# An encoder trunk on one core: the order of all instructions planned with other landing times and durations

## The chip, the cores and the metric

The kernel runs on one core of one Trainium2 chip. A core has a TensorE (PE) for matmuls, a VectorE (DVE), a ScalarE (ACT), a GpSimd (POOL) and a SyncE (SP) that here only issues DMAs. The metric is device time in microseconds (us) of one execution; less is better.

## The reference

Two layers work on x of 256 tokens by 1024. Each is an FFN, a mixer and an FFN, with a layer norm behind each part. The mixer of layer 0 is a bidirectional mLSTM, that of layer 1 a windowed attention with grouped queries.

```python
def swiglu(x, w_in, w_out):
    gu = x @ w_in
    g, u = gu[..., :D_FF], gu[..., D_FF:]
    return (jax.nn.silu(g) * u) @ w_out
...
    for l in range(DEPTH):
        x = layer_norm(ALPHA * x + 0.5 * swiglu(x, ffn_w_in[l, 0], ffn_w_out[l, 0]), ln_g[l, 0], ln_b[l, 0])
        j = l // N_MIXERS
        if l % N_MIXERS == 0:
            y = mlstm_mixer(x, ml_w_in[j], ml_gate_b[j], ml_norm_g[j], ml_w_out[j])
        else:
            y = window_attention(x, at_w_in[j], at_sink[j], at_w_out[j])
        x = layer_norm(ALPHA * x + y, ln_g[l, 1], ln_b[l, 1])
        x = layer_norm(ALPHA * x + 0.5 * swiglu(x, ffn_w_in[l, 1], ffn_w_out[l, 1]), ln_g[l, 2], ln_b[l, 2])
```

All of it is float32, with D_FF = 2816.

## The kernel before

**Products.** A float32 product is made of three matmuls: each operand is split into a high part (a rounded copy, made by ACT, `w_hi` for weights) and a low part (the rest, made by DVE, `w_lo`), and high by high, high by low and low by high are added up in PSUM. Many blocks of the FFN's first product take seven products in place of eight; they need sums of weight blocks. Some of these sums DVE makes (`b <- b, b`), others a DMA makes that adds what it brings to what lies in the tile: 80 accumulating DMAs, all issued by POOL, 512 KB each. A weight tile that was filled that way then goes through ACT (`w_hi <- b`) and DVE (`w_lo <- b, w_hi`) to PE. Plain loads are issued by SP.

**Other names.** `x_69` and `x_70` are the two token tiles of x (called x0 and x1 below). `xT_hi` and `xT_lo` are their transposes, made by PE with `ident` and split by ACT and DVE. A norm takes sums on DVE, the squares on ACT (`sq, sums <- x, sums`), `rs <- sums` on DVE, `rs <- rs, few` on POOL, and two steps on DVE: `x <- x, sums, ln_g` and `x <- x, rs, ln_b`. `h_hi` and `h_lo` are the FFN's inner activation, `e` an evacuated part of a seven-product block, `S` a sum of x's blocks, `q_hi`, `q_lo`, `pr` and `pv` belong to attention.

**The order.** The kernel's text doesn't issue instructions. It notes steps in a `Book`, and `order` plans them: `cost` (L328) gives each step the time that it takes and the time after which its result is seen; `latest` walks from the end and gives each step a due time by what needs it on PE; `sequence` then goes through time and gives each engine, out of the first 16 candidates, one that can start soonest and is due first. For that it must believe when a DMA has landed: `rings.add` models the two queues, with constants in `RING`, `PACKET` and `SUMMED` (L64 to L66), and sets `steps[n_].lands`; `wait_for` decides whether an engine waits a little for a more urgent step. PE's order is that of the text. `sequence` also picks the buffer slot of each tile (10 slots for high parts, 10 for low, 16 for raw weights), so another order gives other slots. `emit` issues the planned list, so that nearly every row of the profile has its line, L597. On the chip every engine runs its own list in order, and waits for semaphores where an operand isn't there yet: a step whose DMA is late holds all that stand behind it on its engine.

Of the kernel before, what the change touches and what calls it, by code (L numbers as in the profile page):

```python
# [11 lines left out]
F32 = mybir.dt.float32  # L12
# [48 lines left out]
LOADING = 1400.0  # L61
ADDING = 5500.0
QUEUED = 6000.0
RING = {"SP": (2000.0, 600.0), "POOL": (2900.0, 1500.0)}  # L64
PACKET = {4096: 162.0, 2048: 88.0, 1024: 48.6}
SUMMED = 163.0  # L66
HELD = 13
PRESSING = 800.0
EARLY = 60000.0
# [96 lines left out]
class Rings:  # L166
# [9 lines left out]
    def run(self, until):  # L176
# [8 lines left out]
        while True:  # L185
# [23 lines left out]
            if not c.left[step]:  # L209
                del c.left[step]  # L210
                if done is not None:
                    done[step] = c.t + RING[q][1]

    def add(self, s, extra=0.0):
# [3 lines left out]
        if q == "POOL":  # L218
            n, each = 16, SUMMED
        else:  # L220
            size = 4 * s.args[1].shape[-1]
            n = max(1, int(np.prod(s.args[0].shape)) * 4 // size // 16)
            each = PACKET.get(size, size / 23.0) + extra / n
        self.jobs[q].append((s.start + RING[q][0], n, each, s.n))
        self.left[s.n] = n
# [24 lines left out]
class Book:  # L250
# [77 lines left out]
    def cost(self, s):  # L328

        size = lambda v: int(np.prod(v.shape[1:]))  # L330
        n = max([size(v) for v in s.outs + s.ins], default=0)
        if s.engine == "PE":
            n = size(s.outs[0])
            s.takes, s.later = (109.0 if s.name == "transpose" else n / 2.4 + 13.3), 200.0
            narrow = s.name == "matmul" and s.args[1].shape[0] == 64
            if narrow:
                s.takes = 58.5
            if narrow != self.narrow:
                s.takes, self.narrow = s.takes + (195.0 if narrow else 146.0), narrow
        elif s.name == "dma_start":  # L340
            s.takes = {"SP": ISSUE, "ACT": 480.0, "POOL": 1250.0}[s.engine]
            s.later = 0.0
        elif s.engine == "DVE":
            psum = any(v.room.kind == "bank" for v in s.ins)
            s.takes, s.later = (n + 71) / 0.96, 120.0
            if s.name == "scalar_tensor_tensor":
                s.takes += 55.0
                if "accum_out" in s.kw:
                    s.takes += 90.0
            if psum and s.outs[0].dtype is F32:  # L350
                s.takes += 60.0
            if s.name == "tensor_add" and s.outs[0].shape[0] == 64:
                s.takes += 30.0
            if s.name == "tensor_tensor_scan":
                s.takes = 710.0
            if s.name == "tensor_tensor_reduce":
                s.takes = 405.0
            if s.name == "bn_stats":
                s.takes = 728.0 if n == 512 else 335.0
            if s.name == "bn_aggr":  # L360
                s.takes = 244.0 if n > 6 else 115.0
        elif s.engine == "ACT":
            s.takes, s.later = n * 0.912 + 17.0, 125.0
            if s.name.startswith("preload"):
                s.takes = 1290.0
            if s.name == "activation" and s.args[2] is not AF.Copy:
                s.takes += 48.0
            if any(isinstance(s.kw.get(k), View) for k in ("bias", "scale")):
                s.takes += 110.0
            if "accum_out" in s.kw:  # L370
                s.takes, s.later = s.takes + 93.0, 215.0
        else:
            s.later = 80.0
            s.takes = {"tensor_tensor": 1500.0, "partition_broadcast": 1100.0, "iota": 600.0,
                       "affine_select": 1600.0}.get(s.name, n * 0.93 + 100.0)
            if s.name == "tensor_add":
                s.takes = 2150.0 if n >= 512 else 1000.0
            if s.name == "tensor_scalar":
                s.takes = 460.0 if n > 64 else 200.0
# [41 lines left out]
    def sequence(self):  # L421
        steps = self.steps
        state = {}
        for kind, rooms in self.rooms.items():
            first, last = np.array([r.first for r in rooms] or [0]), np.array([r.last for r in rooms] or [0])
            n = len(rooms)
# [49 lines left out]
        while len(given) < len(steps):  # L476
            best = None
            for e, list_ in todo.items():
# [7 lines left out]
                for n in cands:  # L486
                    s = steps[n]
# [20 lines left out]
            t, _, n, e = best  # L508
            s = steps[n]
# [8 lines left out]
            if s.name == "dma_start":  # L518
                if e == "POOL" and s.kw.get("accum_op") is None:
                    s.lands = s.end + LANDING + LOADING  # L520
                elif loads < len(RAMP):
                    dma = s.lands = RAMP[loads]
                    rings.t = dma - RING[e][1]
                    loads += 1
                else:
                    for n_, t_ in rings.add(s).items():
                        steps[n_].lands = t_
                        if steps[n_].engine == "SP":
                            dma = max(dma, t_) if n_ == n else dma
                    loads += 1  # L530
# [1084 lines left out]
```

## Time and profile before

| what | us |
|---|---|
| median of 3 runs | 906.04 |
| lowest and highest of them | 904.73, 907.65 |
| the profiled execution | 904.83 |
| its span in the profile | 903.1 |

The profile shows one execution. "Busy" is the time in which an engine runs an instruction; a step's row gives its start, its duration, engine, line, operation and tiles, and in brackets the idle time ahead of it with what ended that. PE's matmuls are pipelined, so the end of one lies behind the start of the next, and stalls are read from the distance of starts. An accumulating DMA shows on POOL only as the 1.2 us in which it is issued; when it landed is told by the table of DMA issues.

### The profile page before, as it was taken

The numbers are of one execution on the slowest core, as the hardware profiler recorded it, in microseconds if no ns is written. First come the engines' busy times: TensorE is split into PE (matmuls) and PEld (weight loads), VectorE is DVE, ScalarE is ACT, GpSimd is POOL, SyncE is SP. The second block draws the span as 40 slices with busy tenths as digits, with TensorE's granted clock in tenths as the row PEclk, the third lists the DMA queues.
The fourth block names the chain that finished last, engine by engine and source line by source line (L and its number), as shares of the span: only waits on it lengthen the run. The fifth ranks groups of instructions, "written<-read, shape, count | busy, mean of one in ns | idle before, by whom it ended". The sixth has DMA issues, their size and how long they took to land.

```text
span 903.1 us, 12618 instructions
## 1 busy us (share of the span) xinstructions
PE 892.5 (99%) x4387; PEld 744.3 (82%) x4387; DVE 815.9 (90%) x1008; ACT 635.1 (70%) x881; POOL 157.8 (17%) x194
## 2 busy tenths in 40 slices
PE   9999999999999999999999999999999999999996
PEld 7888888889988888888888888887898788888885
DVE  7999998678797999999879999996889899999975
ACT  7777677657665886776679776776788777677650
POOL 0121221014012221112011221131033131112100
PEclk9999999999999999999999999999999999999999
DMA  9999998844395989999966999999534588999931
GB/s 317 380 306 273 274 317 243 293 141 141 119 315 149 212 241 316 300 249 278 363 185 177 244 291 322 295 258 347 168 113 113 168 191 230 306 267 263 307 90 46
DMA packets 106111, 216.92 MB, mean 240 GB/s; under 512 B 7192, under 2 KB 23600, under 8 KB 106048
## 3 DMA queue, kind: packets, MB, share of 16 engines
q1 hardware_dynamic: 84000, 174.09, 54.6%
q0 software_dynamic: 22048, 42.04, 27.1%
q8 instruction: 34, 0.56, 0.2%
q14 instruction: 29, 0.24, 0.1%
HBM read 215.04 MB, written 1.05 MB: 239 GB/s over the span
## 4 chain that ended last, share of the span: by engine, by line
PE 73%; DVE 11%; issue 9%; DMA 5%; ACT 1%; POOL 1%; DVEq 0%; POOLq 0%; ACTq 0%
PE pw L597 45%; PE py L597 28%; DVE w_lo L597 5%; DMA b<-in_ffn_w_in_dram 5%; DVE b L597 2%; DVE x L597 1%; DVE e L597 1%; ACT w_hi L597 1%; POOL b L597 1%; POOL rs L597 1%; DVE S L597 0%; DVE xT_lo L597 0%; DVE pv L597 0%; DVE sc L597 0%; DVE h_lo L597 0%
## 5 line engine op out<-in xcount | busy, mean ns | idle before, releaser
L597 ACT CAST w_hi<-b 128x1024 fp32r<-128x1024 f32 x266 | 277.6, 1053 | 98.6 <-PE py L597 45.4
L597 DVE TENSOR_TENSOR w_lo<-b,w_hi 128x1024 fp32r<-128x1024 f32 x266 | 317.5, 1220 | 9.9 <-ACT w_hi L597 9.8
L597 DVE TENSOR_TENSOR w_lo<-raw,w_hi 128x1024 fp32r<-128x1024 f32 (+1 forms) x158 | 187.4, 1208 | 10.5 <-ACT w_hi L597 9.1
L597 PE MATMUL pw<-w_hi,S 128*128 128x512 f32 x608 | 195.3, 391 | 0.2 <-ACT e L597 0.2
L597 ACT CAST w_hi<-raw 128x1024 fp32r<-128x1024 f32 (+1 forms) x158 | 163.2, 1042 | 44.3 <-PE py L597 19.1
L597 POOL DMA_DIRECT2D b<-in_ffn_w_in_dram x80 | 97.0, 1218 | 497.4 <-DVE b L597 173.8
L597 PE MATMUL pw<-w_hi,xT_hi 128*128 128x512 f32 (+1 forms) x420 | 164.9, 394 | 0.4 <-ACT xT_hi L597 0.4
L597 PE MATMUL pw<-w_hi,xT_lo 128*128 128x512 f32 (+1 forms) x420 | 162.4, 388 | 0.0
L597 PE MATMUL pw<-w_lo,xT_hi 128*128 128x512 f32 (+1 forms) x420 | 161.2, 387 | 0.0
L597 PEld LDWEIGHTS pw<-w_hi,S 128*128 128x128 f32 x608 | 114.2, 188 | 25.0 <-ACT e L597 0.7
L597 PE MATMUL py<-w_hi,h_hi 128*128 128x512 f32 x317 | 125.7, 397 | 0.0
L597 PE MATMUL py<-w_hi,h_lo 128*128 128x512 f32 x317 | 124.0, 391 | 0.6 <-DVE h_lo L597 0.6
L597 PE MATMUL py<-w_lo,h_hi 128*128 128x512 f32 x317 | 123.5, 390 | 0.0
L597 PE MATMUL pw<-w_lo,S 128*128 128x512 f32 x304 | 118.4, 390 | 0.0
L597 PEld LDWEIGHTS pw<-w_hi,xT_lo 128*128 128x128 f32 x420 | 78.9, 188 | 18.3 <-DVE xT_lo L597 2.1
L597 PEld LDWEIGHTS pw<-w_hi,xT_hi 128*128 128x128 f32 x420 | 79.0, 188 | 16.2 <-ACT xT_hi L597 1.4
L597 PEld LDWEIGHTS pw<-w_lo,xT_hi 128*128 128x128 f32 x420 | 78.9, 188 | 14.6
L597 DVE TENSOR_TENSOR b<-b,b 128x1024 f32<-128x1024 f32 x72 | 87.7, 1221 | 0.7
L597 PEld LDWEIGHTS py<-w_hi,h_lo 128*128 128x128 f32 x317 | 59.5, 188 | 13.7 <-DVE h_lo L597 1.0
L597 PEld LDWEIGHTS py<-w_lo,h_hi 128*128 128x128 f32 x317 | 59.7, 188 | 11.8
L597 PEld LDWEIGHTS py<-w_hi,h_hi 128*128 128x128 f32 x317 | 59.6, 188 | 11.6
L597 PEld LDWEIGHTS pw<-w_lo,S 128*128 128x128 f32 x304 | 57.1, 188 | 11.6
(205 smaller groups left out, 1102.3 us busy)
## 6 DMA issues: line engine op xcount, KB each, us to landing
b<-in_ffn_w_in_dram SPq DMA_DIRECT2D x152, 512.0 KB, 7.9
raw<-in_ffn_w_out_dram SPq DMA_DIRECT2D x88, 512.0 KB, 8.2
b<-in_ffn_w_in_dram POOLq DMA_DIRECT2D x80, 512.0 KB, 8.8
raw<-in_ml_w_in_dram SPq DMA_DIRECT2D x24, 512.0 KB, 8.0
raw<-in_ffn_w_in_dram SPq DMA_DIRECT2D x36, 256.0 KB, 6.3
raw<-in_at_w_in_dram SPq DMA_DIRECT2D x12, 512.0 KB, 8.6
raw<-in_ml_w_out_dram SPq DMA_DIRECT2D x8, 512.0 KB, 4.5
raw<-in_at_w_out_dram SPq DMA_DIRECT2D x8, 512.0 KB, 8.4
```

Of the source, the lines that this page charges most:

```text
L597: getattr(engines[s.engine], s.name)(*[real(x) for x in s.args], **{k: real(x) for k, x in s.kw.items()})
```

## The change

Constants of the planner change, and one is new. `SPARE` is added to the landing that `sequence` believes of a DMA: 300 ns for SP's and 1500 ns for POOL's, which are the accumulating ones. The ring constants, the price of an accumulating packet and four durations of `cost` change too. No step is added or taken away, and PE's order and SP's order of DMAs stay.

```diff
-RING = {"SP": (2000.0, 600.0), "POOL": (2900.0, 1500.0)}
+RING = {"SP": (2000.0, 1250.0), "POOL": (2900.0, 1150.0)}
+SPARE = {"SP": 300.0, "POOL": 1500.0}
 PACKET = {4096: 162.0, 2048: 88.0, 1024: 48.6}
-SUMMED = 163.0
+SUMMED = 170.0
...
-            s.takes, s.later = (109.0 if s.name == "transpose" else n / 2.4 + 13.3), 200.0
+            s.takes, s.later = (109.0 if s.name == "transpose" else n / 2.4 + (14.3 if n == 512 else 13.3)), 200.0
...
                 if "accum_out" in s.kw:
-                    s.takes += 90.0
-            if psum and s.outs[0].dtype is F32:
-                s.takes += 60.0
+                    s.takes += 30.0
...
             if s.name.startswith("preload"):
-                s.takes = 1290.0
+                s.takes = 1450.0
...
                     for n_, t_ in rings.add(s).items():
-                        steps[n_].lands = t_
+                        steps[n_].lands = t_ + SPARE[steps[n_].engine]
```

Of ACT's 827 steps 150 change their rank, by at most 6; of DVE's 968 steps 251, by at most 14; of POOL's 190 steps 19. Of 1776 tiles 1091 get another slot. In the rows that follow, the number behind a tile's name counts buffers and differs between the two kernels for the same tile; `emit` issues all steps from one line, which is L597 before and L596 now.

First block: ACT in the last FFN, 763 to 774 us in the trace of before. First as it was:

```order
L597 CAST w_hi<-b_7380 128x1024
L597 CAST h_hi<-pw 128x4x128
L597 CAST w_hi<-b_6968 128x1024
L597 CAST w_hi<-b_6980 128x1024
L597 ACTIVATE e_7499<-pw 128x512
L597 CAST w_hi<-b_7082 128x1024
L597 CAST w_hi<-b_7142 128x1024
L597 COPY e_7524<-pw 128x512
L597 CAST w_hi<-b_7390 128x1024
L597 COPY e_7541<-pw 128x512
```

Here b_7082 and b_7142 are the tiles that accumulating DMAs fill, and b_6968 and b_6980 sums that DVE makes; b_7380 and b_7390 belong to the next block. The same place on ACT now, where these tiles are called b_7079 and b_7141, b_6972 and b_6982, b_7377 and b_7387:

```order
L596 CAST w_hi<-b_6972 128x1024
L596 CAST h_hi<-pw 128x4x128
L596 CAST w_hi<-b_7079 128x1024
L596 CAST w_hi<-b_6982 128x1024
L596 ACTIVATE e_7500<-pw 128x512
L596 CAST w_hi<-b_7377 128x1024
L596 COPY e_7517<-pw 128x512
L596 CAST w_hi<-b_7141 128x1024
L596 CAST w_hi<-b_7387 128x1024
L596 COPY e_7543<-pw 128x512
```

The cast of the first accumulated tile moved ahead of the second DVE sum's cast, that of the next block's tile moved back, and the first copy of an e now stands ahead of the cast of the second accumulated tile.

Second block: ACT behind attention, 719 to 724 us, where x0's transposes are split for the last FFN. First as it was:

```order
L597 CAST w_hi<-b_6136 128x1024
L597 CAST w_hi<-b_6187 128x1024
L597 CAST w_hi<-b_6731 128x1024
L597 CAST xT_hi<-py 128x4x128 x2
L597 CAST w_hi<-b_6783 128x1024
L597 ACTIVATE sq,sums<-x_70,sums 128x1024
```

The same place now:

```order
L596 CAST w_hi<-b_6136 128x1024
L596 CAST w_hi<-b_6187 128x1024
L596 CAST xT_hi<-py 128x4x128 x2
L596 CAST w_hi<-b_6732 128x1024
L596 CAST w_hi<-b_6790 128x1024
L596 ACTIVATE sq,sums<-x_70,sums 128x1024
```

Both casts of xT_hi moved ahead of the third weight cast.

Third block: DVE ahead of the third FFN, 290 to 299 us, where x1 (x_70) is normed after the mLSTM. First as it was:

```order
L597 SCALAR_TENSOR_TENSOR x_70,sums<-x_70,py 128x512
L597 TENSOR_SCALAR sums<-sums 128x1 x2
L597 TENSOR_TENSOR w_lo<-b_2437,w_hi 128x1024
L597 TENSOR_TENSOR w_lo<-b_2480,w_hi 128x1024
L597 TENSOR_SCALAR rs<-sums 128x1
L597 SCALAR_TENSOR_TENSOR x_70<-x_70,sums,ln_g 128x1024
L597 SCALAR_TENSOR_TENSOR x_70<-x_70,rs,ln_b 128x1024
L597 TENSOR_TENSOR w_lo<-b_2599,w_hi 128x1024
L597 TENSOR_TENSOR w_lo<-b_2608,w_hi 128x1024
```

The same place now:

```order
L596 TENSOR_TENSOR w_lo<-b_2423,w_hi 128x1024
L596 SCALAR_TENSOR_TENSOR x_70,sums<-x_70,py 128x512
L596 TENSOR_SCALAR sums<-sums 128x1 x2
L596 TENSOR_TENSOR w_lo<-b_2442,w_hi 128x1024
L596 TENSOR_SCALAR rs<-sums 128x1
L596 SCALAR_TENSOR_TENSOR x_70<-x_70,sums,ln_g 128x1024
L596 TENSOR_TENSOR w_lo<-b_2595,w_hi 128x1024
L596 SCALAR_TENSOR_TENSOR x_70<-x_70,rs,ln_b 128x1024
L596 TENSOR_TENSOR w_lo<-b_2604,w_hi 128x1024
```

One w_lo moved ahead of x1's last sum, and another between the two steps of the norm. On ACT a weight cast moved ahead of the squares of x1, and on POOL a DMA moved ahead of rs.

## The prediction

> **What bounds the kernel now.** I read the busy shares first, then the chain that ended last, then a table of stretches, and last the TensorE rows where its matmuls stand apart.
>
> ```profile
> span 903.1 us, 12618 instructions
> PE 892.5 (99%) x4387; PEld 744.3 (82%) x4387; DVE 815.9 (90%) x1008; ACT 635.1 (70%) x881; POOL 157.8 (17%) x194
> PE 73%; DVE 11%; issue 9%; DMA 5%; ACT 1%; POOL 1%; DVEq 0%; POOLq 0%; ACTq 0%
> ```
>
> TensorE (PE) is busy 99% of the span, and in the chain (third line) it has 73%. VectorE (DVE) with 90% is the second engine, and the only other one that could become the bound.
>
> ```profile
> core 0: us, PE busy (x) PEld busy (x) DVE busy (x) ACT busy (x) POOL busy (x), PEclk, DMA share, GB/s
> 460.00:620.00 160.00, 160.00 (x734) 132.38 (x733) 157.22 (x162) 121.86 (x150) 28.65 (x41) 1.00 0.91 261
> 620.00:735.00 115.00, 113.64 (x695) 94.91 (x694) 97.19 (x205) 85.79 (x179) 28.07 (x47) 1.00 0.55 166
> ```
>
> In its first column of busy time PE fills 460 to 620 us wholly, with DVE busy 157.22 of 160 beside it; the attention stretch (620 to 735) lacks 1.36 us. The clock is 1.00 in both. So matmuls are not slowed by a clock, and what an order can win lies in a few small stalls. They show in the starts of successive matmuls:
>
> ```profile
> 773.34 0.39 PE L597 MATMUL py<-w_lo,h_hi 128*128 128x512 f32 x1
> 773.56 0.39 PE L597 MATMUL py<-w_hi,h_lo 128*128 128x512 f32 x1
> 774.19 0.50 PE L597 MATMUL pw<-w_hi,S 128*128 128x512 f32 x1 [0.24 <-ACT e L597]
> ```
>
> Columns are start, duration, engine, line, operation, tiles; the bracket is idle time and its releaser. Starts are about 0.23 us apart when nothing is late (773.34 and 773.56, as rounded), so 774.19 is 0.40 late. In this way I count the other stalls.
>
> ```profile
> 621.14 0.50 PE L597 MATMUL py<-w_hi,h_lo 128*128 128x512 f32 x1 [0.60 <-DVE h_lo L597]
> ...
> 706.67 1.25 PE L597 MATMUL pw<-pr,v 128*128 128x512 f32 x3
> 708.15 0.50 PE L597 MATMUL pw<-pr,v 128*128 128x512 f32 x1 [0.23 <-DVE pr L597]
> ...
> 712.14 0.39 PE L597 MATMUL py<-w_lo,q_hi 128*128 128x512 f32 x1
> 712.68 0.50 PE L597 MATMUL py<-w_hi,q_lo 128*128 128x512 f32 x1 [0.15 <-DVE q_lo L597]
> ...
> 721.33 0.40 PE L597 MATMUL py<-w_hi,q_lo 128*128 128x512 f32 x1
> 721.89 0.50 PE L597 MATMUL pw<-w_hi,xT_hi 128*128 128x512 f32 x1 [0.16 <-ACT xT_hi L597]
> 722.23 0.40 PE L597 MATMUL pw<-w_lo,xT_hi 128*128 128x512 f32 x1
> 722.62 0.50 PE L597 MATMUL pw<-w_hi,xT_lo 128*128 128x512 f32 x1
> ```
>
> Three starts after 706.67 the next would be due at 707.36: 0.79 late at 708.15. By the same step 712.68 is 0.31 late, 721.89 0.33 and 722.62 0.16. Behind such a stop the next start comes a little later too: 722.23 is 0.34 after 721.89, 0.1 more than the rule. With the 0.40 at 774.19, about 0.1 for the restart behind each of five, and the one stall that the order leaves alone (0.60 in the bracket at 621.14), some 3.1 us are in sight. Even if all of it went, the kernel would gain 0.35%: the bounds of this change lie narrow on the good side and open on the bad one. A measurement of this kernel tells about 0.3%, 2.7 us, from no change.
>
> [...]
>
> **The change part by part.** It takes no instruction away and adds none; DMAs keep their order on SP. Only the planner's picture of time changes, so ACT, DVE and POOL get some rows in another order and tiles other buffers. The edited durations (a matmul 1 ns longer, an evacuation 60 ns shorter, a table load 160 ns longer) cost nothing themselves: the chip takes what it takes. What they and the later landings bring is the order, and most of its moves lie in stretches like 460 to 620 us, where PE has no hole: weights are ready there ahead of their matmuls. Those I cost at nothing, hidden by the matmuls that PE still has to do; where that cover is gone, a moved step costs its own length, some 1.05 us for a cast (765.83) and 1.22 for a low half (767.81, below). At four places a move meets a thin margin.
>
> *The last FFN, 763 to 774 us (the first order block).*
>
> ```profile
> 765.83 1.06 ACT L597 CAST w_hi<-b 128x1024 fp32r<-128x1024 f32 x1 [0.33 <-PE pw L597]
> ...
> 771.17 1.05 ACT L597 CAST w_hi<-b 128x1024 fp32r<-128x1024 f32 x1 [2.86 <-DMA b<-in_ffn_w_in_dram]
> 772.12 0.57 ACT L597 COPY e<-pw 128x512 f32<-128x512 f32 x1
> ...
> 773.55 0.58 ACT L597 COPY e<-pw 128x512 f32<-128x512 f32 x1
> ```
>
> ACT stood 2.86 us idle behind a cast whose accumulating DMA had not landed, and the two e copies came after it; the second ended at 774.13 and PE's matmul started at 774.19. Now the first e copy stands ahead of the waiting cast, in its idle time. The second copy then ends one copy's length earlier, nearly 0.5 us (0.57 in its row, of which some lies beside the next): at about 773.65, ahead of the due 773.79. The stall of 0.40 and its 0.10 go: −0.5 us. But the first of the two casts that wait for accumulating DMAs moves ahead too, past a cast of plain sums that ran at 765.83.
>
> ```profile
> b<-in_ffn_w_in_dram POOLq DMA_DIRECT2D x1, 512.0 KB, 10.7
> 756.33 1.20 POOL L597 DMA_DIRECT2D b<-in_ffn_w_in_dram  x1 [13.59 <-DVE b L597]
> 767.81 1.22 DVE L597 TENSOR_TENSOR w_lo<-b,w_hi 128x1024 fp32r<-128x1024 f32 x1
> 769.94 0.39 PE L597 MATMUL pw<-w_lo,S 128*128 128x512 f32 x1
> ```
>
> Its DMA, issued at 756.33, took 10.7 us (the DMA issues of 756 to 758 us, first line), so it landed at 767.0. With that landing the waiting cast runs to 768.05, the one behind it to 769.1, its low half on DVE to 770.3, and the matmul that used it at 769.94 waits 0.4. Here the change adds a wait with a queue behind it. If the DMA took the median below, 8.8 us, it would land at 765.1 and the wait would be gone. Together −0.5 to +0.4; I take the same landing: −0.5 + 0.4 = **−0.1 us**.
>
> *The first matmul after attention, 719 to 722 us (second order block).*
>
> ```profile
> 719.36 2.00 ACT L597 CAST w_hi<-b 128x1024 fp32r<-128x1024 f32 x2 [0.79 <-PE py L597]
> 721.27 1.06 ACT L597 CAST xT_hi<-py 128x512 fp32r<-128x512 f32 x2
> ```
>
> The two xT_hi casts ran behind the second of two weight casts; now they run ahead of it, from about 720.4, when half of the first row's 2.00 is over. The first is done near 721.0 (half of 1.06 each), and PE, due at 721.56, finds it: 0.33 and the restart's 0.10 go. The low half comes from DVE, whose place hardly moves, so the 0.16 at 722.62 stays or grows to 0.3 now that PE gets there earlier. **−0.35 us**, between −0.45 and −0.2.
>
> *Inside attention, 705 to 713 us.* ACT gets q_hi and a weight cast ahead of the pr casts; I estimate that pr ends 0 to 0.2 later, which adds to the 0.79. DVE gets q_lo and pv ahead of a weight, which can take half or all of the 0.31 at 712.68. **−0.1 us**, between −0.3 and +0.2.
>
> *The norm of x1 ahead of the third FFN, 291 to 298 us (third order block).*
>
> ```profile
> 291.91 1.14 ACT L597 ACTIVATE sq<-x,sums 128x1024 bf16<-128x1024 f32 x1
> ...
> 293.55 1.28 DVE L597 SCALAR_TENSOR_TENSOR x<-x,sums,ln_g 128x1024 f32<-128x1024 f32 x1
> 295.29 1.29 DVE L597 SCALAR_TENSOR_TENSOR x<-x,rs,ln_b 128x1024 f32<-128x1024 f32 x1 [0.47 <-POOL rs L597]
> 293.73 1.53 POOL L597 TENSOR_TENSOR rs<-rs,few 128x1 f32<-128x1 f32 x1
> 298.14 1.03 PE L597 MATMUL py<-ident,x 128*128 128x128 f32 x8
> 726.38 2.35 DVE L597 TENSOR_TENSOR w_lo<-b,w_hi 128x1024 fp32r<-128x1024 f32 x2
> 726.53 2.63 POOL L597 TENSOR_TENSOR rs<-rs,few 128x1 f32<-128x1 f32 x1
> ```
>
> Before, x1 was normed by 296.58 and PE transposed it at 298.14, 1.56 us later. Three moves use that up. ACT casts a weight ahead of the squares of x1 (1.05 later); POOL issues a DMA (1.2 us) ahead of rs; and DVE makes a weight's low half between the two steps of the norm. The squares, which ended at 293.05, now end near 294.1, the gain step at 295.5, the weight at 296.6. POOL's rs would end 1.53 after its DMA, at 296.4, and the norm would end at 297.9, in time. But rs has been seen to wait for DVE: at 726.53 it took 2.63 us and ended at 729.16, 0.43 behind the two weights that DVE ran till 728.73. With that, rs ends at 297.05, the norm at 298.35, and the transposes start 0.3 late. Between 0 and +0.5 (0.1 for the restart); nearest is the row at 726 us with the same neighbours: **+0.3 us**.
>
> [...]
>
> **Sum**: −0.1 − 0.35 − 0.1 + 0.3 = −0.25 us, its ends −1.25 and +0.9. The profiled execution took 904.83 us with a span of 903.1; the sum makes it 904.6. The median of the three runs (906.04) lay 1.21 above the profiled one, so the forecast is 905.8, its own range 904.8 to 907.
>
> **The rivals.**
>
> ```profile
> b<-in_ffn_w_in_dram POOLq DMA_DIRECT2D x80, 512.0 KB, 8.8
> ACT w_hi L597 <- DMA b<-in_ffn_w_in_dram: 19.3, 22, 2.9
> ```
>
> *Late landings are planned for, and the stalls go.* ACT waited 22 times, 19.3 us in all (second line), for the weights' DMAs, at most 2.9 us at once; the new plan has an accumulating DMA land some 1.5 us later than the old one, so it covers more of those that take longer than the median of 8.8 (first line). Runs without the profiler reach 907.65, 2.9 above the lowest, and if later landings in them make that difference, an order that holds against them wins it, beside the stalls of attention and the last FFN. Then it is 906.04 less 2.0 (0.40, 0.79, 0.31, 0.33 and 0.16) to 4.4 (all 3.1 in sight, and the 1.31 from the median down to the lowest run): 901.6 to 904.0, say 902.8. Against it: PE, which sets the end, shows only 0.5 us behind a landing.
>
> *Casts queue behind a landing where margins are thin (slower).* ACT takes its rows in order, so a cast put forward onto an accumulating DMA holds all casts behind it. Between 460 and 620 us DVE is busy 98% and cannot make up: each microsecond that ACT is held passes to PE once the weight's margin is used, and in the trace the margin is 0.9 us at 769.94 (1.22 after 767.81, against 769.94). From a landing of 10.7 us on, the cast at 769 us costs 0.4; a landing of 12.5 us, 1.8 more, costs 2.2 there. Two such make +4: 910. Against it: of the 80 such casts 25 stand later in ACT's order than before and 7 earlier.
>
> *The change does nothing that matters.* All moves lie in margins, as at most of the places, and the stalls keep their sizes: 906.0.
>
> **How the numbers follow.** The forecast has 0.48, the rival that does nothing 0.12, the one in which stalls and late landings go 0.23, the slower one 0.17. The first two lie within 0.3% (903.3 to 908.8); I give same 0.60, faster 0.23, slower 0.17. To leave out no more than two in ten, the range goes down to 902.6, about the middle of the faster rival, and up to 908.8.
>
> **What would show it.** In the new profile: the stall at 774 us gone and a wait of 0.2 to 0.4 us for a w_lo near 770; at 721.9 no wait on xT_hi; at 298 transposes 0.2 to 0.4 late, with rs longer than 2 us; PE without holes between 460 and 620. I am wrong if PE stalls by more than 1 us at a place where it had none, above all behind a cast that waits for a DMA, or if the stalls stay and the time falls all the same.

## The result, and the profile after

| | before | changed |
|---|---|---|
| median of 5 runs, us | 906.04 | 911.20 |
| lowest and highest | 904.37, 907.65 | 910.23, 913.27 |
| profiled execution, us | 904.83 | 910.23 |
| its span | 903.1 | 908.5 |

The changed kernel is slower: ratio 1.0065, 95% interval 1.0043 to 1.0087. The profile's first lines and its line on the chain hardly tell why:

```profile
span 908.5 us, 12627 instructions
PE 894.7 (98%) x4387; PEld 747.2 (82%) x4387; DVE 815.5 (90%) x1008; ACT 635.6 (70%) x881; POOL 156.8 (17%) x194
PE 86%; DVE 8%; issue 2%; ACT 2%; DMA 1%; DVEq 0%; POOL 0%; ACTq 0%
```

DVE, ACT and POOL are as busy as before, and PE 2.2 us more, though it does the same matmuls. The view of PE's waits (engine, tile, releaser: total, times, longest) names the place:

```profile
PE pw L596 <- DVE h_lo L596: 4.2, 2, 4.0
```

One wait of 4.0 us for an h_lo, where before no wait behind the start was longer than 0.6. The timeline of PE shows it at the end of the first FFN's seven-product blocks:

```profile
137.94 0.39 PE L596 MATMUL py<-w_hi,h_lo 128*128 128x512 f32 x1
142.30 0.80 PE L596 MATMUL pw<-w_hi,xT_hi 128*128 128x512 f32 x1 [3.97 <-DVE h_lo L596]
142.89 0.63 PE L596 MATMUL pw<-w_lo,xT_hi 128*128 128x512 f32 x1
143.32 0.63 PE L596 MATMUL pw<-w_hi,xT_lo 128*128 128x512 f32 x1
```

The start due at 138.17 comes at 142.30, 4.13 late. And then the matmuls start 0.43 us apart, not 0.23. The table of stretches (its eighth field is the granted clock) says why:

```profile
core 0: us, PE busy (x) PEld busy (x) DVE busy (x) ACT busy (x) POOL busy (x), PEclk, DMA share, GB/s
140.00:141.00 1.00, 0.00 (x0) 0.00 (x0) 0.79 (x2) 1.00 (x3) 0.00 (x0) 0.98 0.00 0
141.00:147.60 6.60, 5.30 (x13) 4.14 (x14) 6.60 (x7) 3.44 (x4) 1.77 (x2) 0.50 0.15 17
147.60:148.20 0.60, 0.60 (x4) 0.52 (x3) 0.32 (x1) 0.37 (x1) 0.60 (x2) 0.84 0.89 253
```

PE stood still, its clock fell to half near 141.0, and it came back near 147.8 (from 0.84 in the last stretch: half clock for 0.19 of its 0.60). The twelve steps from start to start that follow are together 2.5 us longer than in the kernel of before, and the one after them 0.1; of these 2.6 us some 0.1 is the restart (in the fifth experiment, where the clock stayed at 1.00, the second start behind the stop comes 0.34 us after the first, 139.27 and 139.61, not 0.23), so the clock's part is 2.5. Matched start by start, PE in the two traces is 0.6 us apart at 137 us and 7.3 at 148: the hole and the clock behind it cost 6.7 us, more than the whole difference of the spans (5.4). Beside it 0.7 us came in the first 8 us: 0.2 where PE waited for x's own load, and 0.5 as the slow matmuls of the start (0.3 to 0.6 us from start to start) went on till 7.96 us, and till 7.04 before. Another 0.5 came at 371 us; 2.4 were won between 628 and 781 us, of which more below.

What PE waited for is told by the chain of waits of the changed kernel from 126 to 143 us (start, length, what):

```profile
126.74 0.49 POOL b L596
...
127.47 10.41 DMA few<-in_ml_w_in_dram
...
137.96 0.57 ACT gw L596 x4
138.54 1.89 ACT w_hi L596 x2
140.43 0.50 ACT g L596
...
140.95 0.51 DVE e L596
...
141.56 0.69 DVE h_lo L596
...
142.30 0.80 PE pw L596
```

Read from the end: PE needed h_lo done (h_lo reads the PSUM bank that the next block writes); DVE's h_lo stands behind an e that needs ACT's g, and needs ACT's h_hi itself; and ACT stood in its row before the four small gw casts, which come ahead of both, until a plain load of 64 KB, the mLSTM's gate weights, had landed. PE needs gw only at 202.9 us here (195.54 before). The load is issued by POOL, and there the order has changed. POOL's timeline, first before, then changed:

```profile
123.98 1.21 POOL L597 DMA_DIRECT2D b<-in_ffn_w_in_dram  x1 [11.49 <-PE py L597]
124.71 1.42 POOL L597 DMA_DIRECT2D few<-in_ml_w_in_dram  x1
127.57 1.18 POOL L597 DMA_DIRECT2D b<-in_ffn_w_in_dram  x1 [1.44 <-DVE b L597]
```

```profile
124.58 1.21 POOL L596 DMA_DIRECT2D b<-in_ffn_w_in_dram  x1 [11.57 <-PE py L596]
126.74 1.20 POOL L596 DMA_DIRECT2D b<-in_ffn_w_in_dram  x1 [0.96 <-DVE b L596]
127.47 1.42 POOL L596 DMA_DIRECT2D few<-in_ml_w_in_dram  x1
```

The small load and the second accumulating DMA have changed places. The load is issued 2.8 us later, behind two accumulating DMAs rather than one, and its landing takes 10.4 us instead of 7.9 (DMA issues, before and changed):

```profile
few<-in_ml_w_in_dram POOLq DMA_DIRECT2D x1, 64.0 KB, 7.9
```

```profile
few<-in_ml_w_in_dram POOLq DMA_DIRECT2D x1, 64.0 KB, 10.4
```

So ACT's gw casts start at 137.96 and not at 132.72. There the old trace had shown how near it was:

```profile
132.72 0.58 ACT L597 CAST gw<-few 128x32 fp32r<-128x32 f32 x4 [2.48 <-DMA few<-in_ml_w_in_dram]
136.66 0.69 DVE L597 TENSOR_TENSOR h_lo<-pw,h_hi 128x512 fp32r<-128x512 f32 x1
137.60 0.40 PE L597 MATMUL pw<-w_hi,xT_hi 128*128 128x512 f32 x1
```

ACT had stood 2.48 us for this load before the change too, and h_lo ended (137.35) 0.25 us ahead of the matmul that needed its bank. No margin was left, and the load came 5.2 us later.

Why POOL's row changed is told by the times that `order` plans. A plain load of POOL may start 60 us ahead of its due time: 124.21 us in the old plan, 125.00 in the new, since PE's planned matmuls are 1 ns longer each. The accumulating DMA was planned at 125.80 and is now at 124.73, as DVE's work ahead of it was reordered around later landings. Either shift alone leaves the load first (125.00 against 125.80, 124.21 against 124.73); both together swap them.

### The profile page after: what moved, and what is told of

Read it like the earlier page. It is cut to its first block, busy times and chain, and to the rows that moved or that the text cites. A ratio compares the mean times of both kernels' runs of the same rounds, so it can differ in the third digit from the quotient of the medians.

```text
span 908.5 us, 12627 instructions
## 1 busy us (share of the span) xinstructions
PE 894.7 (98%) x4387; PEld 747.2 (82%) x4387; DVE 815.5 (90%) x1008; ACT 635.6 (70%) x881; POOL 156.8 (17%) x194
## 3 DMA queue, kind: packets, MB, share of 16 engines
HBM read 215.04 MB, written 1.05 MB: 238 GB/s over the span
## 4 chain that ended last, share of the span: by engine, by line
PE 86%; DVE 8%; issue 2%; ACT 2%; DMA 1%; DVEq 0%; POOL 0%; ACTq 0%
PE pw L596 54%; PE py L596 32%; DVE w_lo L596 4%; DVE b L596 1%; DMA few<-in_ml_w_in_dram 1%; ACT w_hi L596 1%; DVE x L596 1%; DVE e L596 0%; DVE S L596 0%; DVE pr L596 0%; DMA x<-in_x_dram 0%; DVE pv L596 0%; DVE h_lo L596 0%; ACT xT_hi L596 0%; DVE few L596 0%
## 5 line engine op out<-in xcount | busy, mean ns | idle before, releaser
L596 ACT CAST w_hi<-b 128x1024 fp32r<-128x1024 f32 x266 | 277.7, 1053 | 98.8 <-PE py L596 54.0
L596 DVE TENSOR_TENSOR w_lo<-b,w_hi 128x1024 fp32r<-128x1024 f32 x266 | 317.4, 1219 | 14.5 <-ACT w_hi L596 14.5
L596 DVE TENSOR_TENSOR w_lo<-raw,w_hi 128x1024 fp32r<-128x1024 f32 (+1 forms) x158 | 187.2, 1207 | 11.3 <-ACT w_hi L596 9.8
L596 PE MATMUL pw<-w_hi,S 128*128 128x512 f32 x608 | 195.1, 390 | 0.3 <-DVE h_lo L596 0.3
L596 ACT CAST w_hi<-raw 128x1024 fp32r<-128x1024 f32 (+1 forms) x158 | 162.9, 1042 | 37.5 <-PE pw L596 19.4
L596 POOL DMA_DIRECT2D b<-in_ffn_w_in_dram x80 | 96.9, 1216 | 493.8 <-DVE b L596 188.6
L596 PE MATMUL pw<-w_hi,xT_hi 128*128 128x512 f32 (+1 forms) x420 | 165.8, 396 | 4.2 <-DVE h_lo L596 4.0
L596 PE MATMUL pw<-w_hi,xT_lo 128*128 128x512 f32 (+1 forms) x420 | 163.6, 391 | 0.0
L596 PE MATMUL pw<-w_lo,xT_hi 128*128 128x512 f32 (+1 forms) x420 | 162.0, 389 | 0.0
L596 PEld LDWEIGHTS pw<-w_hi,S 128*128 128x128 f32 x608 | 114.1, 188 | 25.0 <-DVE h_lo L596 1.2
L596 PE MATMUL py<-w_hi,h_hi 128*128 128x512 f32 x317 | 125.6, 396 | 0.0
L596 PE MATMUL py<-w_hi,h_lo 128*128 128x512 f32 x317 | 123.8, 391 | 0.0
L596 PE MATMUL py<-w_lo,h_hi 128*128 128x512 f32 x317 | 123.4, 389 | 0.0
L596 PE MATMUL pw<-w_lo,S 128*128 128x512 f32 x304 | 118.3, 389 | 0.0
L596 PEld LDWEIGHTS pw<-w_hi,xT_hi 128*128 128x128 f32 x420 | 79.6, 190 | 20.1 <-DVE h_lo L596 4.4
L596 PEld LDWEIGHTS pw<-w_hi,xT_lo 128*128 128x128 f32 x420 | 79.7, 190 | 18.6 <-DVE xT_lo L596 2.1
L596 PEld LDWEIGHTS pw<-w_lo,xT_hi 128*128 128x128 f32 x420 | 79.4, 190 | 14.8
L596 DVE TENSOR_TENSOR b<-b,b 128x1024 f32<-128x1024 f32 x72 | 87.7, 1220 | 0.8
L596 PEld LDWEIGHTS py<-w_hi,h_lo 128*128 128x128 f32 x317 | 59.5, 188 | 12.9 <-DVE h_lo L596 0.3
L596 PEld LDWEIGHTS py<-w_lo,h_hi 128*128 128x128 f32 x317 | 59.7, 188 | 11.8
L596 PEld LDWEIGHTS py<-w_hi,h_hi 128*128 128x128 f32 x317 | 59.7, 188 | 11.7
L596 PEld LDWEIGHTS pw<-w_lo,S 128*128 128x128 f32 x304 | 57.1, 188 | 11.6
```

Source lines behind the costliest of these rows:

```text
L596: getattr(engines[s.engine], s.name)(*[real(x) for x in s.args], **{k: real(x) for k, x in s.kw.items()})
```

## The experiments

Twelve kernels ran; each edit is small. In those that move single steps, 1111 is the small load, 933 the second accumulating DMA, 1248 to 1254 the four gw casts, 1044, 1022 and 992 weight casts of ACT. In the edits `given` is the planned list of steps and `at` finds a step's place in it. "Before" in a ratio is the kernel of before beside it on the same chip (medians 905.06 to 905.17).

**1. The load put back.** In the changed kernel:

```diff
+        given.insert(at(933), given.pop(at(1111)))
```

> The changed kernel, in which only POOL's small load of the gate weights (64 KB) is issued again ahead of the accumulating DMA of 126.7 us, as before the change. Theory (the load's place on POOL holds ACT's four gw casts till 137.96, ACT holds PE for 4.1 us, and the clock that falls in that hole costs 2.5 more): gw casts near 133, no hole at 142, clock 1.00 throughout, 911.2 - 6.6 = 904.6, so 1 to 2 under the kernel of before. Rival 1 (the swap is an accident beside another cause in the moved casts of ACT or DVE): a hole of several us stays near 140, 908 to 911. Rival 2 (the hole goes, and another opens as the accumulating DMA is now later): 906 to 908.

Measured: 904.56 us (903.78 to 905.13), ratio to before 0.9995 (0.9986 to 1.0004). PE's row at the place, in the timeline of this kernel:

```profile
137.53 0.39 PE L599 MATMUL py<-w_hi,h_lo 128*128 128x512 f32 x1
137.75 0.39 PE L599 MATMUL pw<-w_hi,xT_hi 128*128 128x512 f32 x1
```

No hole. One instruction moved by one place takes the whole loss away.

**2. The casts moved back.** In the changed kernel, POOL's row untouched:

```diff
+        for n in (1248, 1250, 1252, 1254):
+            given.insert(at(1044), given.pop(at(n)))
```

> The changed kernel with POOL's order as it is there, and ACT's four gw casts moved back behind the cast of the second accumulated tile, some 7 steps later (PE needs them at 195 us). Theory (the landing does harm only because ACT's casts wait for it at their place in the row): the load still lands near 138, ACT does not wait for it, no hole, 904.6 as with the loads put back. Rival (the small load holds the accumulating DMAs or the tiles themselves, whatever ACT does): a hole of over 2 us stays, 908 or more.

Measured: 904.51 us (902.77 to 905.92), ratio 0.9993 (0.9984 to 1.0001). There is no hole: the last matmul of the block ahead starts at 137.65, the next one at 137.88. The load still took 10.5 us. So the late landing harms only through the place of ACT's casts.

**3. The swap in the kernel of before.** The line is that of the first experiment; here the load stands ahead, so it goes behind the DMA.

```diff
+        given.insert(at(933), given.pop(at(1111)))
```

> The kernel of before with one edit: POOL issues the accumulating DMA of 127.57 ahead of the small load of 124.71. Theory: the load is issued near 128.3 and lands near 138.7; ACT waits until then, PE for about 4.9 us, and the clock falls as in the changed kernel: 906 + 4.9 + 2.5 = 913.5 (911.5 to 914.5). Rival (another part of the change makes the hole): 906, no hole.

Measured: 911.81 us (911.62 to 913.74), ratio 1.0078 (1.0064 to 1.0092). PE and ACT in its timeline:

```profile
142.25 0.79 PE L600 MATMUL pw<-w_hi,xT_hi 128*128 128x512 f32 x1 [4.13 <-DVE h_lo L600]
```

```profile
137.91 0.57 ACT L600 CAST gw<-few 128x32 fp32r<-128x32 f32 x4 [7.31 <-DMA few<-in_ml_w_in_dram]
```

The loss without the change. The load landed 0.9 us earlier than I had put it (9.2 us after its issue), so the hole is 4.3 us rather than 4.9.

**4. One constant undone.** In the changed kernel a 512-wide matmul is planned without the extra 1 ns:

```diff
-            s.takes, s.later = (109.0 if s.name == "transpose" else n / 2.4 + (14.3 if n == 512 else 13.3)), 200.0
+            s.takes, s.later = (109.0 if s.name == "transpose" else n / 2.4 + 13.3), 200.0
```

> The changed kernel with one constant of the planner undone: a 512-wide matmul planned with 13.3 ns over its columns again, all other edits kept. By the plan this moves the small load's earliest time 0.8 us forward, ahead of the accumulating DMA again, and little else. Theory: no hole, 904 to 905.5. Rival (the later landings of accumulating DMAs themselves cost, by casts that queue): 907 or more with holes behind casts that wait for a DMA.

Measured: 904.54 us (904.17 to 905.51), ratio 0.9991 (0.9982 to 1.0001). The later landings, with which I had worked out most terms, do no harm by themselves: they are all still in this kernel.

**5 and 6. A shorter hole.** In the changed kernel the casts go behind step 1022 (two weight casts later), or behind 992 (one):

```diff
+        for n in (1248, 1250, 1252, 1254):
+            given.insert(at(1022), given.pop(at(n)))
```

> The changed kernel with the four gw casts moved back by two weight casts only, so that ACT has less to do once the small load has landed near 138: h_lo ends near 140.3 and PE stands still for about 2.2 us instead of 4.1. Theory (the clock falls only after more than 2.4 us without matmuls, as the two holes of 4.1 us show it at 141.0 and 140.6): clock 1.00 throughout, cost 2.2 + 0.1, so 904.5 + 2.3 = 906.8. Rival (any hole of over 1 us takes the clock down): 2.5 more, 909.3.

> The same with the gw casts moved back by one weight cast only: PE stands still for about 3.2 us. Theory (half clock begins 2.4 to 2.7 us after the last matmul and lasts some 5 us from the next on): 904.5 + 3.2 + 2.5 = 910.2. Rival 1 (the clock falls only behind a hole of 3.4 us or more): 907.8. Rival 2 (the time at half clock grows with the hole): between them, 908.5 to 909.5.

Measured: 908.11 us (906.33 to 908.19; ratio 1.003, 1.0017 to 1.0042) and 908.97 us (908.4 to 910.49; ratio 1.0049, 1.0037 to 1.0062). PE in the timeline of the fifth, then of the sixth:

```profile
136.95 0.39 PE L600 MATMUL py<-w_hi,h_lo 128*128 128x512 f32 x1
139.27 0.50 PE L600 MATMUL pw<-w_hi,xT_hi 128*128 128x512 f32 x1 [1.93 <-DVE h_lo L600]
139.61 0.39 PE L600 MATMUL pw<-w_lo,xT_hi 128*128 128x512 f32 x1
```

```profile
136.98 0.39 PE L600 MATMUL py<-w_hi,h_lo 128*128 128x512 f32 x1
140.33 0.50 PE L600 MATMUL pw<-w_hi,xT_hi 128*128 128x512 f32 x1 [2.96 <-DVE h_lo L600]
...
141.42 0.63 PE L600 MATMUL pw<-w_lo,xT_hi 128*128 128x512 f32 x1
141.85 0.63 PE L600 MATMUL pw<-w_hi,xT_lo 128*128 128x512 f32 x1
```

A hole of 2.1 us left the clock alone (1.00 in each stretch from 138 to 147 us): the start after the hole comes 0.34 behind it, one slow step, and the duration is 0.39 again. A hole of 3.1 us took it down, later than I had thought, 0.9 us after the matmuls had begun again, and for a shorter time (stretches of the sixth kernel):

```profile
141.00:142.00 1.00, 1.00 (x5) 0.76 (x4) 1.00 (x2) 0.51 (x1) 0.00 (x0) 0.64 0.00 0
142.00:144.00 2.00, 2.00 (x7) 1.51 (x6) 2.00 (x3) 1.56 (x2) 1.16 (x1) 0.50 0.00 0
144.00:145.00 1.00, 1.00 (x4) 0.83 (x3) 1.00 (x2) 0.03 (x1) 0.10 (x1) 0.65 0.65 57
```

By the shares in the first and the last row, half clock from 141.28 to 144.70, which is 3.4 us. The 6.8 us of the changed kernel are twice that. The sixth time, 908.97, lies where the second rival had it, and not at the 910.2 of the theory.

The fifth kernel was 1.3 us slower than expected, and its trace holds the reason at another place, the first one of the prediction: PE stood at 772 and 773 us.

```profile
772.39 0.50 PE L600 MATMUL pw<-w_hi,S 128*128 128x512 f32 x1 [0.48 <-ACT w_hi L600]
773.65 0.50 PE L600 MATMUL pw<-w_lo,S 128*128 128x512 f32 x1 [0.76 <-DVE w_lo L600]
```

The accumulating DMA took 12.3 us here (8.9 in the profile of the changed kernel, 10.5 in the second experiment, both without a hole there), and the casts queued behind it as the slower rival had said, for some 1.7 us.

**7 and 12. The other places.** The profile of the second experiment has one more hole of the new order: 1.3 us at 366 us, for an h_lo that DVE makes behind a weight's low half which PE needs later. The seventh kernel moves that h_lo (2713) ahead of the low half (2775). The twelfth also puts the cast of the first accumulated tile of the last FFN (5889) back behind that of the second DVE sum and the activation after it (5833). Both keep the edit of the second experiment.

```diff
+        given.insert(at(2775), given.pop(at(2713)))
+        given.insert(at(5833), given.pop(at(5889)))
```

> The changed kernel with the gw casts moved back as in the second run (no hole at 142 there), and one more edit: on DVE the h_lo of 365.3 us goes ahead of a weight's low half that PE needs 4 us later. Theory (the 1.2 us that PE waits for h_lo at 366 are DVE's order alone, a loss of the new plan): that wait falls to 0.2 or less, 904.5 - 1.1 = 903.4. Rival (the low half that steps back is late then, or the landing of its tile holds it): 904.5 or more.

> The kernel with both holes closed (gw casts late, h_lo early), and the cast of the first accumulated tile of the last FFN put back behind the cast of the second DVE sum, where it stood before the change. Theory (runs near 905 of the kernel with two edits are those in which that tile lands over 12 us after its issue and the casts queue behind it, as in the profile of the half-way casts at 772): the same best, 902.3, and few runs over 904.2; median 903.0 to 903.6. Rival (the scatter comes from elsewhere, such as the start): as with two edits, 903.9 and runs to 905.5.

Measured: 903.90 us (902.33 to 905.5), ratio 0.9987 (0.9978 to 0.9996); and 902.62 us (901.71 to 903.12), ratio 0.9975 (0.9965 to 0.9985). The first gain is 0.6 us where 1.1 were expected: the hole at 366 went, and half a us came at 418, where PE waits for another h_lo. The second narrowed the runs from 3.2 to 1.4 us and took 1.3 off the median, more than expected; the two intervals still overlap. That fits casts that queue behind a landing in some runs, but it isn't shown: only the profiled runs were traced, in neither of those two does PE stand still at 770 us, and of the 0.9 us between them 0.4 come in the first 8 us. So the rival, by which the scatter comes from the start, isn't excluded. The twelfth kernel beats both: it stands 2.4 us under before, the changed one 5.2 over it.

**8, 10 and 11. The parts alone**, each on the kernel of before: SPARE; the four planned durations; the ring constants with SUMMED. The edits are the lines of the diff of the change.

> The kernel of before with SPARE added and nothing else changed, that is only the later landings in the plan. POOL's small load stays ahead of the accumulating DMA in that plan. Theory (the hole needs SPARE and the longer matmul together; SPARE alone only trades stalls): no hole at 142, 904 to 906. Rival (later landings in the plan make casts queue behind landings): 907 or more, with waits of ACT for DMAs that PE feels.

> The kernel of before with only the four planned durations of the change. By the plan the small load comes 0.8 us later than before and still ahead of the accumulating DMA. Theory (no part alone makes the hole): 904 to 906. Rival (the longer matmul is enough, by the 0.8 us): a hole near 138 and 907 or more.

> The kernel of before with only the ring constants and the price of an accumulating packet changed. Theory (no part alone makes the hole): 904 to 906. Rival: a hole of its own, 907 or more.

Measured: 905.45 us (904.46 to 906.6), ratio 1.0001 (0.9992 to 1.001); 907.56 us (905.68 to 910.42, and one run of 3187 that I can't explain), ratio 1.0029 (1.0015 to 1.0044); 906.21 us (905.4 to 907.99), ratio 1.0018 (1.0009 to 1.0027). None has the hole at 138. But the durations alone aren't free, as I had expected them to be, and the ring constants cost some 1 us, too. PE's longest waits behind the start, in the profile of the durations:

```profile
PE py L595 <- DVE h_lo L595: 1.4, 1, 1.4
PE pw L595 <- ACT e L595: 1.1, 2, 0.6
PE pw L595 <- DVE h_lo L595: 1.1, 2, 0.9
```

Matched with before, the kernel of the durations loses 5.6 us between 319 and 447 us; the changed kernel, which has these durations too, loses 0.6 on that stretch. The parts don't add up.

**9. The landing told to the planner.** In the changed kernel:

```diff
-                    s.lands = s.end + LANDING + LOADING
+                    s.lands = s.end + 9200.0
```

> The changed kernel with one more constant of the planner set to the trace: a plain load that POOL issues is planned to land 9.2 us after its issue ends (10.4 us were seen) in place of 3.6. The new plan puts the gw casts six steps later on ACT, behind h_hi and one more cast, and POOL's order stays as in the changed kernel. Theory (the plan's belief about this one landing is what put the casts where they hold ACT): no hole at 142, 904.5 as with the casts moved by hand. Rival (a planner that is told of one landing opens a hole elsewhere): 906 or more.

Measured: 904.18 us (902.77 to 905.16), ratio 0.9992 (0.9984 to 1.0001). ACT's row:

```profile
137.04 0.67 ACT L596 CAST gw<-few 128x32 fp32r<-128x32 f32 x4 [0.78 <-DMA few<-in_ml_w_in_dram]
```

The casts wait 0.78 us and hold nobody. The change had corrected the landings of the loads that run through the ring model and left the one that doesn't: planned to land 3.6 us after the end of its issue, it landed 9.0 after it in the changed kernel (10.4 from the start of an issue of 1.42).

## Why the prediction was wrong, point by point

**The step that failed** is "most of its moves lie in stretches like 460 to 620 us, where PE has no hole ... Those I cost at nothing, hidden by the matmuls that PE still has to do". At 138 us the cover was 0.25 us. The margin that I had measured ran from a weight's low half to its matmul, in the last FFN (0.9 us); what PE lacked in the first FFN was a PSUM bank, which h_lo sets free. And I had weighed moves by their own length, 1.05 us for a cast: the move that mattered was of a DMA on POOL, whose landing moved by 5.2 us. What was put at nothing cost 6.7 us there, and the swap alone brings that loss and takes it away (experiments 1 and 3). So the prediction's own sign of being wrong came: a stall of more than 1 us where PE had none, behind a cast that waits for a DMA.

**The rest of the sum.** Without the hole (experiments 1, 2 and 4) the changed kernel takes 904.51 to 904.56, some 0.6 under before, though the intervals just include no change; I had −0.25. That the two lie near each other is luck. As the terms below show, two came out some 0.4 better than forecast, and the +0.3 of a third did not come; and the stall at 621, which went, and the losses in the first 8 us and at 371 (0.7 and 0.5) were no terms of mine.

**What bounds it.** Right that PE does, and that the bad side was open. But "a clock" was put aside, since it was 1.00 in the stretches before the change; behind the holes of 3.1, 4.1 and 4.3 us it was 0.50 for 3.4, 6.8 and 6.8 us. In the changed kernel that put 2.5 us on top of the hole.

**The last FFN.** The stall of 0.40 went, as said, and with the restart 0.5 us. The new one of 0.4 near 770 did not come in the profile, where the DMA took 8.9 us. It took 10.5 in the second experiment, and there was still none; 10.8 in the sixth, and a matmul on a w_lo came 0.17 us late (774.46); 12.3 in the fifth, and 1.7 us came. So the mechanism was right, and the 0.4 at 10.7 somewhat too much.

**After attention.** Right: in the changed kernel no wait on xT_hi, and 0.19 left on xT_lo.

```profile
728.33 0.39 PE L596 MATMUL pw<-w_hi,xT_hi 128*128 128x512 f32 x1
728.56 0.40 PE L596 MATMUL pw<-w_lo,xT_hi 128*128 128x512 f32 x1
728.98 0.50 PE L596 MATMUL pw<-w_hi,xT_lo 128*128 128x512 f32 x1
```

**Inside attention.** Better than −0.1: matched start by start, 0.5 us went between 705 and 713 us of before. Nearly all of it is the stall on q_lo (712.68), which went with its restart; the one on pr moved by a matmul and lost 0.1. The stall on h_lo at 621, which I had left standing, went too (0.76).

**The norm of x1.** Wrong by its whole size: +0.3 was forecast, nothing came. DVE, POOL and PE of the changed kernel, in which these rows come 7.5 us later:

```profile
301.67 1.27 DVE L596 SCALAR_TENSOR_TENSOR x<-x,sums,ln_g 128x1024 f32<-128x1024 f32 x1
302.86 1.22 DVE L596 TENSOR_TENSOR w_lo<-b,w_hi 128x1024 fp32r<-128x1024 f32 x1
304.00 1.27 DVE L596 SCALAR_TENSOR_TENSOR x<-x,rs,ln_b 128x1024 f32<-128x1024 f32 x1
```

```profile
301.92 1.45 POOL L596 TENSOR_TENSOR rs<-rs,few 128x1 f32<-128x1 f32 x1
```

```profile
305.37 0.39 PE L596 MATMUL pw<-w_hi,xT_lo 128*128 128x512 f32 x1
305.60 1.03 PE L596 MATMUL py<-ident,x 128*128 128x128 f32 x8
```

rs took 1.45 us and ended at 303.37, while DVE's next w_lo (302.86, 1.22 us) was running; x1 was normed by 305.27, and PE's transposes start 0.23 us behind the matmul ahead of them, without a wait. Taking the row at 726 us as the pattern was the error: beside a w_lo on DVE rs took 2.63 us there and 1.45 here, as far as spans on POOL, which are rough, tell it. That rs waits for DVE, on which the +0.3 rested, this row does not show.

**The rivals.** The slower one named ACT held by a landing, and that is what happened, but with the wrong landing (an accumulating DMA's) and at the wrong place. As it counted casts of accumulated tiles only, the four gw casts weren't among them. "The change does nothing that matters" fell. The faster one had its first half right: ACT waits for the weights' DMAs 15 times and 11.0 us in the changed kernel, where it was 22 times and 19.3 us; but PE had felt little of these waits, and the hole outweighed them. Its time, 902.8, is reached only by the twelfth kernel.

## What to carry to other kernels

A row that waits for a DMA is as dangerous as all the rows behind it are urgent: go through every load that an in-order engine waits for, small plain ones too, and compare its landing with the margin of what stands behind. Margins are to be taken for every resource that PE needs, banks as well as operands. And a planner that is corrected in some costs only can lose more than it gains, since its order jumps with each of them; afterwards look for the one new hole in the trace and move that step.

## What was not expected of the hardware

With a hole of 2.1 us PE kept its clock (1.00, the fifth experiment); with one of 3.1 us (the sixth) it ran at half clock for 3.4 us, and with 4.1 us (the changed kernel) and 4.3 us (the third experiment) for 6.8. The clock fell at different times: 2.6 us after the last matmul's end at 138.33 in the changed kernel, but 3.9 after 137.37 in the sixth experiment, when PE was already at work again.

The rows and the clock show what lies around each fall. In the 3.4 us ahead of it, as long as half clock lasted in the sixth experiment, PE had stood still for 2.63 us in the changed kernel (the fall at 140.96), 2.46 in the sixth (141.28) and 2.44 in the third (140.56). In the fifth, where the clock stayed, it stood still for 1.93 us in all, from the last end at 137.34 to the start at 139.27. In the changed kernel and the third experiment PE stood still for 1.3 and 1.7 us behind the fall too, and half clock lasted 6.8 us; in the sixth PE was at work again by then, and it lasted 3.4. Times without matmuls between 1.93 and 2.44 us were not tried.

The times have a common measure. Half clock lasted 6.827 us in the clock records of the changed kernel, and the records of full clock ahead of it and behind it last 133.120 and 757.759 us, from 7.84 and from 147.79 on. In the kernel before, the record of full clock begins at 6.54 and lasts 894.292 us. These are 39.0, 222.0 and 262.0 times half of 6.827. What makes it so the runs don't show.

A 64 KB load on POOL's queue took 7.9 us behind one accumulating DMA of 512 KB (before) and 10.4 behind two (the changed kernel); in the first experiment, behind one again, it took 7.3, and behind two 10.5 in the second and 9.2 in the third. It landed 0.3 us after the accumulating DMA issued just ahead of it before (132.64 behind 132.35) and 0.5 us after it in the changed kernel (137.88 behind 137.42).
